# The moving tiles of a weight-stream kernel, stored as even and odd tokens and read in turn

## The chip, the cores and the metric

The kernel runs on one core of a Trainium2 chip. The metric is the device time of one execution, in microseconds. Three runs of the kernel before are shown, with a median of 1940.2 us. One execution was taken by the hardware profiler; all rows of the profile come from it.

The core has five instruction queues that matter here: TensorE (PE, with its weight loads listed as PEld), VectorE (DVE), ScalarE (ACT), GpSimd (POOL) and SyncE (SP), which issues most DMAs.

## The reference

One inference step of one decoder layer, for a prompt of 256 tokens and eight sample tokens of one step each. All is float32. Cut to the products with the large weights:

```python
mod = silu(c) @ w_ada + b_ada                      # 2048 -> 6 x 2048
h = rmsnorm(x) * (1 + sc1) + sh1
z = h @ w_in                                       # 2048 -> 15376
y_a = spatial_gating(u, v)                         # three mixers, each 1024 wide
y_b = head_rmsnorm(o_hg) * silu(hg)
y_c = head_rmsnorm(o_gla) * silu(gr)
merged = sum(sigmoid(z_gate[n]) * (y[n] @ w_branch[n]) for n in range(3))
x = x + gt1 * rmsnorm(merged @ w_out)
h2 = rmsnorm(x) * (1 + sc2) + sh2
x = x + gt2 * rmsnorm(square(relu(h2 @ w_mlp_up)) @ w_mlp_down)
```

The two mixers b and c are gated linear recurrences with states that are also outputs.

## The kernel before, in words

Activations are held with features on the 128 partitions and tokens along the free dimension. A block is a tile of 128 partitions x 4 feature groups x 264 tokens (`NT` = 256 prompt tokens, `NP`, and 8 samples, `NS`), made by `blk`. A product with a large weight takes a 128x128 piece of the weight as the stationary operand and 128x264 activations as the moving operand, and adds up in PSUM.

To be nearly exact, each float32 operand is split into a high part, rounded to the chip's fast float32 type (`F32R`), and a low part, the rest. `split` (lines 108 to 110) does this with a copy on Scalar and a subtraction on Vector. A product is then three: high weight x high activation, high weight x low activation, low weight x high activation (lines 643, 644 and 645, in `granule`).

The weights come as a stream. `plan` lists all pieces in the order of use, `Stream.load` issues their DMAs on SP into `raw` tiles (four buffers, with a few in `araw`), up to five pieces ahead. `Stream.split_half` splits them into `whi` and `wlo` (six buffers each), up to two pieces ahead. `granule` does the 24 products of one piece, and `background` then lets a share of the other work run: generators of the three mixers (`mixer_a`, `samples_r`, `mixer_r`), the modulation rows (`Rounds`), and work that was put off (`later`). The order on TensorE, and in some stages on other queues, is that of the program text.

The activations that the stream multiplies are split as follows:

- `modulate` (lines 425 to 453) makes `h` in pairs of feature groups and splits it into `hh` and `hl`. The first pair goes feature group by feature group, its samples on GpSimd (lines 430 to 434), its first prompt part on Vector (lines 447 and 448). `hH` and `hL` hand one feature group of it to `granule`.
- `yparts` (line 1308) splits the gated outputs of mixers a and b, `parts_c` (line 1363) those of mixer c.
- `branch` (line 1318) gates the projected mixers with tanh(z / 2) + 1, which is twice the sigmoid, and sums them in `mg`. The missing factor of 0.5 is put in when `mg` is split (lines 1337 and 1338).
- `quad` and `put_quad` (lines 1545 to 1580) make and split `h2`, its samples on GpSimd.
- `up` (line 1605) squares the positive part of the MLP's first product; its high part comes straight from Scalar's square (line 1616), its low part from Vector. `down` uses it one block of 1024 features later.

`tiles` (line 709) hands out the feature group `k` of a list of such blocks. Each moving operand is thus 264 tokens in a row, 1056 bytes on each partition:

```python
def tiles(bl):
    return lambda k: bl[k // 4][:, k % 4, :]
```

The factor of two of the other gates (`gate_tiles`, line 1342) is made good in the norm gains `hgnT` and `glanT`, which are multiplied by 0.5 at the start (line 163).

Of the kernel before, what the change touches and what calls it, by code (L numbers as in the profile page):

```python
# [57 lines left out]
def hybrid_step_kernel(  # L58
# [40 lines left out]
    def mul(o, a, b):  # L99
        V.tensor_tensor(o, a, b, op=ALU.mult)  # L100
# [7 lines left out]
    def split(src, hi, lo):  # L108
        S.copy(hi, src)  # L109
        sub(lo, src, hi.bitcast(F32))  # L110

    order = tc.manual_schedule(engines={mybir.EngineType.PE, mybir.EngineType.SP, mybir.EngineType.Pool})
    order.__enter__()

# [43 lines left out]
    def small_vectors():  # L158
        ps = sm()
        T.transpose(ps[:, 0:128], st1, ident)  # L160
        T.transpose(ps[:, 128:128 + n2], st2[0:n2, :], ident[0:n2, 0:n2])
        V.tensor_copy(vec, ps[:, 0:128 + n2])
        V.tensor_scalar(vec[:, 172:175], vec[:, 172:175], 0.5, None, ALU.mult)

    badaT = vec[:, 0:96]
    gpreT, gpostT = vec[:, 96:112], vec[:, 112:128]
# [258 lines left out]
    def modulate(dst, src, xs, k0, n, A, B, hi, lo):  # L425

        d = dst[:, :, NP:NT]
        one = k0 == 0
        if one:
            Q = nc.gpsimd  # L430
            Q.tensor_tensor(d, xs[:, k0:k0 + n, :], A[:, k0:k0 + n, 1:NC], op=ALU.mult)
            Q.tensor_tensor(d, d, B[:, k0:k0 + n, 1:NC], op=ALU.add)
            Q.tensor_copy(hi[:, :, NP:NT], d)
            Q.tensor_tensor(lo[:, :, NP:NT], d, hi[:, :, NP:NT].bitcast(F32), op=ALU.subtract)
        else:
            mul(d, xs[:, k0:k0 + n, :], A[:, k0:k0 + n, 1:NC])
            add(d, d, B[:, k0:k0 + n, 1:NC])
        for j in range(n):
            k = k0 + j
            if j % 2 == 0:  # L440
                V.tensor_scalar(dst[:, j, 0:NP], src[:, j, :], A[:, k, 0:1], B[:, k, 0:1], ALU.mult, ALU.add)
            else:
                S.activation(dst[:, j, 0:NP], src[:, j, :], AF.Identity, scale=A[:, k, 0:1], bias=B[:, k, 0:1])
            if one:
                p, h, l = (b[:, j, 0:NP] for b in (dst, hi, lo))
                if j == 0:
                    V.tensor_copy(h, p)
                    sub(l, p, h.bitcast(F32))
                else:
                    split(p, h, l)  # L450
            elif j % 2 == 1:
                js = slice(j - 1, j + 1)
                split(dst[:, js, :], hi[:, js, :], lo[:, js, :])

    hh, hl = [], []
    A1 = const([P, KT, NC], "A1")
# [250 lines left out]
        return acc[:, 0:width // P, 0:NT]  # L707

    def tiles(bl):
        return lambda k: bl[k // 4][:, k % 4, :]  # L710

    def pair(b, g):
        return b[:, 2 * g:2 * g + 2, :]

    def hH(k):
        return hh[k // 4][:, k % 4, :]

    def hL(k):
        return hl[k // 4][:, k % 4, :]

    win = w_in[0]

# [142 lines left out]
    def mixer_a():  # L865
        lng, lnb, wsr, bsb = consts_a
        lng, lnb = (v.rearrange("p g n -> p (g n)") for v in (lng, lnb))
        vtk = [blk([P, BW]), blk([P, BW])]
        yield from rows_of(vF, lambda t, g: vtk[t][:, g * CW:(g + 1) * CW])
        wsT = blk([P, 8, P])  # L870
        w00 = tmp([P, 8], "w00", 1)
        for gg in range(2):
            ps = sm()
            for i in range(4):
                T.transpose(ps[:, i * P:(i + 1) * P], wsr[:, 4 * gg + i, :], ident)
            yield
            mul(wsT[:, 4 * gg:4 * gg + 4, :], ps.rearrange("p (g n) -> p g n", g=4), triu.unsqueeze(1).to_broadcast([P, 4, P]))
        yield READY
        ps = sm()
        T.matmul(ps[:, 0:8], ones[0:1, :], wsT[0:1, :, 0:1].rearrange("p g o -> p (g o)"), start=True, stop=True)  # L880
        V.tensor_copy(w00, ps[:, 0:8])
        yield
        for v in vtk:
            st = tmp([P, 2, 6], "bst", 1)
            for i in range(2):
                V.bn_stats(st[:, i, :], v[:, i * 512:(i + 1) * 512])
            ag = tmp([P, 2], "bag", 1)
            V.bn_aggr(ag, st)
            rs = tmp([P, 1], "lnr", 1)
            rstd_small(ag[:, 1:2], 1.0, rs)  # L890
            yield
            V.tensor_scalar(v, v, ag[:, 0:1], rs, ALU.subtract, ALU.mult)
            yield
            mul(v, v, lng)
            yield
            add(v, v, lnb)
            yield

        vs = tmp([P, 8, NS], "vsa", 1)
        w8 = tmp([P, 8, NS], "vsb", 1)  # L900
        r8 = tmp([P, NS], "vsr", 1)
        for i in range(2):
            V.tensor_copy(vs[:, 4 * i:4 * i + 4, :], vF[i][:, :, NP:NT])
        V.tensor_copy(w8, vs)
        fold(w8, 8)
        yield READY
        ps = sum_partitions(w8, NS)
        yield 0.3
        V.tensor_scalar(r8, ps, 1.0 / BW, None, ALU.mult)
        sub(vs, vs, r8.unsqueeze(1).to_broadcast([P, 8, NS]))  # L910
        mul(w8, vs, vs)
        fold(w8, 8)
        yield 0.3
        yield READY
        ps = sum_partitions(w8, NS)
        yield 0.1
        rstd_small(ps, 1.0 / BW, r8)
        mul(vs, vs, r8.unsqueeze(1).to_broadcast([P, 8, NS]))
        mul(vs, vs, lngT.unsqueeze(2).to_broadcast([P, 8, NS]))
        add(vs, vs, lnbT.unsqueeze(2).to_broadcast([P, 8, NS]))  # L920
        V.tensor_copy(srow[:, 0:8, :].rearrange("p k b -> p (k b)").rearrange("p (b k) -> p k b", k=8), vs)
        yield 0.9
        yield READY
        yield READY
        ps = sm([P, P])
        T.transpose(ps, srow.rearrange("p k b -> p (k b)"), ident)
        so = tmp([64, P], "sqs", 1)
        S.copy(so, ps[0:64])
        nc.gpsimd.dma_start(sgu_v_sample[0].rearrange("b o (k p) -> (b o k) p", p=P), so)
        ys = tmp([P, 8, NS], "vsb", 1)  # L930
        mul(ys, vs, w00.unsqueeze(2).to_broadcast([P, 8, NS]))
        add(ys, ys, bsb[:, :, 0:1].to_broadcast([P, 8, NS]))
        for i in range(2):
            u = uT[i][:, :, NP:NT]
            mul(u, ys[:, 4 * i:4 * i + 4, :], u)
        yield 0.8
        for gp in range(4):
            ps = sm()
            for i in range(2):
                g = 2 * gp + i  # L940
                for c in range(2):
                    T.matmul(ps[:, (2 * i + c) * P:(2 * i + c + 1) * P], vtk[c][:, g * P:(g + 1) * P], wsT[:, g, :], start=True, stop=True)
            u = pair(uT[gp // 2], gp % 2)
            yv = tmp([P, 2, NT], "vt")
            yield
            add(
                yv[:, :, 0:NP].rearrange("p g (c n) -> p g c n", c=2),
                ps.rearrange("p (g c n) -> p g c n", g=2, c=2),
                bsb[:, 2 * gp:2 * gp + 2, :].unsqueeze(2).to_broadcast([P, 2, 2, P]),
            )  # L950
            mul(u[:, :, 0:NP], yv[:, :, 0:NP], u[:, :, 0:NP])
            yield
    order = tc.manual_schedule(engines={mybir.EngineType.PE, mybir.EngineType.Pool})
    order.__enter__()
# [353 lines left out]
    def yparts(ys):  # L1308
        h, l = [], []
        for y in ys:  # L1310
            a, b = blk(dt=F32R), blk(dt=F32R)
            split(y, a, b)
            h.append(a)
            l.append(b)
            bg.owed -= 0.8
        return tiles(h), tiles(l)

    def branch(n, parts):
        for m in range(8):
# [14 lines left out]
                add(dst, dst, gt)  # L1334
            if n == 2 and m % 2 == 1:
                a, b = blk(dt=F32R), blk(dt=F32R)
                S.activation(a, mg[m // 2], AF.Copy, scale=0.5)
                V.scalar_tensor_tensor(b, mg[m // 2], 0.5, a.bitcast(F32), ALU.mult, ALU.subtract)
                mh.append(a)
                ml.append(b)  # L1340

# [21 lines left out]
    def parts_c(gates):  # L1363
# [3 lines left out]
        for j, o in enumerate(Gs[2].o):  # L1367
# [1 line left out]
                g = gates[hd // 2][:, 2 * (hd % 2) + j, :]  # L1369
                V.scalar_tensor_tensor(o[:, hd, :], o[:, hd, :], glanT[:, j:j + 1], g, ALU.mult, ALU.mult)  # L1370
            a, b = blk(dt=F32R), blk(dt=F32R)
            split(o, a, b)
            h.append(a)
            l.append(b)
            bg.owed -= 0.8
        return (lambda k: h[k % 2][:, k // 2, :]), (lambda k: l[k % 2][:, k // 2, :])

    rate[:] = RATES[1]
    branch(0, parts_a)
# [164 lines left out]

    def quad(q):

        hs, ls = (h[q][:, :, NP:NT] for h in (h2h, h2l))
        Q.tensor_copy(hs, xa[:, 4 * q:4 * q + 4, :])
        Q.tensor_tensor(ls, xa[:, 4 * q:4 * q + 4, :], hs.bitcast(F32), op=ALU.subtract)
        for i2 in range(2):  # L1550
            if q > 0:
                ps = sm([P, 2, NP])
# [18 lines left out]
    def put_quad(q, i2, i, src, vt):  # L1571
# [5 lines left out]
        if q == 0 or i == 1:  # L1577
            a = i if q == 0 else 0
            js = slice(2 * i2 + a, 2 * i2 + i + 1)
            split(vt[:, a:i + 1, 0:NP], h2h[q][:, js, 0:NP], h2l[q][:, js, 0:NP])  # L1580

    quad(0)
    residual(1)
# [21 lines left out]
    def up(f, zs=()):  # L1605
        ah, al = [], []
        for m in range(FB // CW):
# [5 lines left out]
                al.append(blk(dt=F32R))  # L1613
            a, b = pair(ah[-1], m % 2), pair(al[-1], m % 2)
            sq = tmp([P, 2, NT], "gt")
            S.activation(a, rl, AF.Square)
            mul(sq, rl, rl)
            sub(b, sq, a.bitcast(F32))
        return tiles(ah), tiles(al)

    y2 = [blk() for _ in range(4)]
# [123 lines left out]
```

## Time and profile before

| | before |
|---|---|
| median of 3 runs | 1940.2 us |
| lowest and highest run | 1939.84 and 1943.49 us |
| span of the profiled execution | 1941.0 us |
| mean granted TensorE clock | 0.998 |
| products with 264 columns | 3 x 4624 |
| HBM read and written | 427.60 and 11.70 MB |

The page gives no time around the span, so the span is taken as the profiled execution's own time; it lies between the lowest and the highest run. A group's row reads: line, engine, operation, output<-inputs, shapes, count | busy time in us, mean ns of one | idle time of the engine before them and what ended it. Products overlap in the array, so the mean of one is not the distance to the next. A row of stretches reads: from:to, length, then busy time and count on TensorE, its weight loads, Vector, Scalar and GpSimd, then the granted clock, the mean share of the DMA engines and GB/s. A row in order of time reads: start, duration, engine, line, operation and how many instructions were merged into it.

### The profile page before, as it was taken

The page shows a single profiled execution, that of the slowest core. Times are in us where ns is not written, and L with a number is a line of the kernel's source. Part 1 is how long each engine was busy: PE and PEld are TensorE (multiplying, and loading weights), DVE is VectorE, ACT ScalarE, POOL GpSimd, SP SyncE. Part 2 cuts the span into 40 slices and gives each one's busy share as a digit, 9 for nine tenths or more (in the row PEclk, how much of TensorE's full clock was granted, in tenths as well). Part 3 has the DMA queues.
Part 4 walks back from the last instruction along what each step waited for, and adds up shares of the span by engine and source line. Part 5 has one row for each costly group of instructions (what it writes and reads, how often), then busy time and mean ns, then how long its engine had stood idle before and what let it go on. Part 6 is the DMA issues. An engine that isn't in the chain of part 4 may idle for free.

```text
span 1941.0 us, 42183 instructions
## 1 busy us (share of the span) xinstructions
PE 1906.3 (98%) x17012; PEld 1815.6 (94%) x17012; DVE 1186.7 (61%) x2092; ACT 1002.7 (52%) x1818; POOL 130.9 (7%) x210
## 2 busy tenths in 40 slices
PE   6999999999999999999999999999999999999998
PEld 5899999999999989899999989999999999999997
DVE  4566667686676785555555666545556555555665
ACT  5434354665855755544444555444444545454544
POOL 4311000001101111100000010000000000000000
PEclk9999999999999999999999999999999999999999
DMA  9987696788777778877777846776556556555552
GB/s 338 372 303 252 193 299 205 226 263 258 232 253 243 235 254 265 288 257 249 259 247 234 304 131 201 233 228 196 177 182 184 179 180 184 177 183 180 180 184 100
DMA packets 330179, 442.05 MB, mean 228 GB/s; under 512 B 14946, under 2 KB 276944, under 8 KB 329984
## 3 DMA queue, kind: packets, MB, share of 16 engines
q1 hardware_dynamic: 311728, 380.26, 61.7%
q0 software_dynamic: 17184, 57.85, 8.5%
q8 instruction: 133, 2.18, 0.5%
q10 hardware_dynamic: 1072, 1.25, 0.2%
q14 instruction: 62, 0.51, 0.1%
HBM read 427.60 MB, written 11.70 MB: 226 GB/s over the span
## 4 chain that ended last, share of the span: by engine, by line
PE 93%; DMA 3%; DVE 1%; issue 1%; ACT 1%; SPq 0%; POOL 0%; DVEq 0%; ACTq 0%; POOLq 0%
PE mm L643 28%; PE mm L644 28%; PE mm L645 28%; PE ada L362 3%; DMA raw<-in_w_in_dram 1%; PE ada L294 1%; DMA vbc<-vs_d 1%; PE sm L835 1%; PE sm L663 1%; DVE wlo L106 1%; PE sm L1192 1%; PE sm L670 1%; DMA b<-in_x_prompt_dram 0%; PE sm L1562 0%; DMA b<-in_w_ada_dram 0%
## 5 line engine op out<-in xcount | busy, mean ns | idle before, releaser
L643 PE MATMUL mm<-b,whi 128*128 128x264 f32 x4624 | 1326.4, 287 | 8.3 <-issue 2.4
L645 PE MATMUL mm<-b,wlo 128*128 128x264 f32 x4624 | 1313.1, 284 | 3.9 <-DVE wlo L106 3.6
L644 PE MATMUL mm<-b,whi 128*128 128x264 f32 x4624 | 1314.3, 284 | 0.6 <-DVE b L106 0.5
L106 DVE TENSOR_TENSOR wlo<-raw,whi 128x512 fp32r<-128x512 f32 x1136 | 776.9, 689 | 568.4 <-ACT whi L109 564.9
L109 ACT CAST whi<-raw 128x512 fp32r<-128x512 f32 x1136 | 696.2, 618 | 750.9 <-PE mm L644 669.2
L643 PEld LDWEIGHTS mm<-b,whi 128*128 128x128 f32 x4624 | 870.7, 188 | 49.6 <-issue 28.2
L645 PEld LDWEIGHTS mm<-b,wlo 128*128 128x128 f32 x4624 | 870.5, 188 | 5.1 <-DVE wlo L106 5.1
L644 PEld LDWEIGHTS mm<-b,whi 128*128 128x128 f32 x4624 | 871.0, 188 | 2.8 <-issue 1.4
L103 DVE TENSOR_TENSOR b<-b,mm 128x528 f32<-128x528 f32 (+1 forms) x137 | 95.7, 699 | 40.2 <-PE mm L645 39.9
L1089 DVE SCALAR_TENSOR_TENSOR st<-vbc,b,st 128x128 f32<-128x128 f32 (+1 forms) x96 | 34.1, 390 | 62.2 <-DMA vbc<-vs_d 57.4
L1087 ACT ACTIVATE st<-st,fs 128x128 f32<-128x128 f32 (+1 forms) x96 | 37.1, 431 | 56.4 <-DMA st<-in_state_hgrn_dram 28.6
L472 POOL DMA_DIRECT2D b<-in_w_ada_dram x64 | 46.2, 724 | 132.4 <-PE ada L294 101.3
L362 PE MATMUL ada<-araw,cT 128*32 128x512 f32 x296 | 39.8, 601 | 0.0
L294 PE MATMUL ada<-b,cT 128*32 128x256 f32 (+1 forms) x640 | 34.9, 354 | 1.8 <-DMA b<-in_w_ada_dram 1.5
L100 DVE TENSOR_TENSOR b<-b,b 128x512 f32<-128x512 f32 (+1 forms) x47 | 33.8, 740 | 1.3 <-ACT b L1205 1.1
L1090 POOL DMA_DIRECT2D out_dram<-st x32 | 23.5, 736 | 130.0 <-DVE st L1089 130.0
L294 PEld LDWEIGHTS ada<-b,cT 128*32 128x32 f32 x640 | 17.7, 113 | 14.3 <-DMA b<-in_w_ada_dram 5.3
L362 PE MATMUL ada<-b,cT 128*32 128x512 f32 x216 | 26.2, 593 | 0.0
L106 DVE TENSOR_TENSOR b<-gt,b 128x528 fp32r<-128x528 f32 x32 | 22.7, 708 | 3.2
L106 DVE TENSOR_TENSOR b<-b 128x1024 f32<-128x1024 f32 (+1 forms) x24 | 24.3, 1015 | 0.0
L109 ACT CAST whi<-araw 128x512 fp32r<-128x512 f32 x20 | 12.3, 620 | 21.0 <-PE mm L644 17.6
L100 DVE TENSOR_TENSOR gt<-vt 128x528 f32<-128x528 f32 x32 | 22.5, 702 | 0.9 <-ACT vt L1610 0.9
(346 smaller groups left out, 859.1 us busy)
## 6 DMA issues: line engine op xcount, KB each, us to landing
raw<-in_w_in_dram SPq DMA_DIRECT2D x231, 512.0 KB, 4.6
raw<-in_w_mlp_up_dram SPq DMA_DIRECT2D x128, 512.0 KB, 3.9
raw<-in_w_mlp_down_dram SPq DMA_DIRECT2D x128, 512.0 KB, 3.6
araw<-in_w_ada_dram SPq DMA_DIRECT2D x74, 512.0 KB, 5.4
b<-in_w_ada_dram SPq DMA_DIRECT2D x54, 512.0 KB, 5.5
b<-in_w_ada_dram POOLq DMA_DIRECT2D x48, 512.0 KB, 8.0
raw<-in_w_branch_dram SPq DMA_DIRECT2D x48, 512.0 KB, 4.5
raw<-in_w_out_dram SPq DMA_DIRECT2D x32, 512.0 KB, 4.0
```

What stands on the lines that cost most here:

```text
L100: V.tensor_tensor(o, a, b, op=ALU.mult)
L103: V.tensor_tensor(o, a, b, op=ALU.add)
L106: V.tensor_tensor(o, a, b, op=ALU.subtract)
L109: S.copy(hi, src)
L294: T.matmul(acc[32 * j:32 * j + 32, 0:n], cT[:, k, :], w[:, n * j:n * j + n], start=k == 0, stop=k == KT - 1)
L362: T.matmul(self.acc[32 * j:32 * j + 32, :], cT[:, k, :], ws[j // 2][:, j % 2 * 512:j % 2 * 512 + 512], start=k == 0, stop=k == KT - 1)
L472: queue.dma_start(w[:, i], w1[k * P:(k + 1) * P, :, self.k0 * P:(self.k0 + self.n) * P])
L643: T.matmul(o, a, xh(k + j), start=first and j == 0, stop=False)
L644: T.matmul(o, a, xl(k + j), start=False, stop=False)
L645: T.matmul(o, b, xh(k + j), start=False, stop=last and j == n - 1)
L1087: S.activation(st[:, i, :], st[:, i, :], AF.Copy, scale=fs[:, h0 + i, b:b + 1])
L1089: V.scalar_tensor_tensor(st[:, i, :], v[:, i, :], k[:, h0 + i, NP + b:NP + b + 1], st[:, i, :], ALU.mult, ALU.add)
```

## The change

A moving tile's 264 tokens are stored in two halves of 132 words: the even tokens, then the odd ones. `apart` views a stored tile as its two halves, `by_two` views a source by even and odd tokens, and `split_tokens` splits a source of natural order into parts stored that way. `moving` gives the products a view that takes a token from the first half and one from the second half in turn, so the columns of a product, and what it writes to PSUM, have the order of before. Tokens 0 to 255 and the samples fill columns 0 to 127 and 128 to 131 of each half.

All makers of moving parts write this way. Weights, their split and all sources stay as they are. Since the split of `mg` no longer scales, its 0.5 is moved ahead: into the gated values of mixer a (the products become a product of three factors, one of them 0.5) and into `hgnT` and `glanT` (0.25 in place of 0.5). `up` takes its high part with the same views.

```diff
+    def apart(v):
+        return v.rearrange("p n (r c) -> p n r c", r=2)
+
+    def by_two(v):
+        return v.rearrange("p n (c r) -> p n r c", r=2)
+
+    def moving(v):
+        return v.rearrange("p (r c) -> p c r", r=2)
+
+    def split_tokens(src, hi, lo, t0=0, t1=NT):
+
+        cs = slice(t0 // 2, t1 // 2)
+        split(by_two(src), apart(hi)[:, :, :, cs], apart(lo)[:, :, :, cs])
...
-        V.tensor_scalar(vec[:, 172:175], vec[:, 172:175], 0.5, None, ALU.mult)
+        V.tensor_scalar(vec[:, 172:175], vec[:, 172:175], 0.25, None, ALU.mult)
...
-            Q.tensor_copy(hi[:, :, NP:NT], d)
-            Q.tensor_tensor(lo[:, :, NP:NT], d, hi[:, :, NP:NT].bitcast(F32), op=ALU.subtract)
+            hs, ls = (apart(b)[:, :, :, NP // 2:NT // 2] for b in (hi, lo))
+            Q.tensor_copy(hs, by_two(d))
+            Q.tensor_tensor(ls, by_two(d), hs.bitcast(F32), op=ALU.subtract)
...
-                p, h, l = (b[:, j, 0:NP] for b in (dst, hi, lo))
+                p = by_two(dst[:, j:j + 1, 0:NP])
+                h, l = (apart(b[:, j:j + 1, :])[:, :, :, 0:NP // 2] for b in (hi, lo))
...
-                split(dst[:, js, :], hi[:, js, :], lo[:, js, :])
+                split_tokens(dst[:, js, :], hi[:, js, :], lo[:, js, :])
...
     def tiles(bl):
-        return lambda k: bl[k // 4][:, k % 4, :]
+        return lambda k: moving(bl[k // 4][:, k % 4, :])
...
     def hH(k):
-        return hh[k // 4][:, k % 4, :]
+        return moving(hh[k // 4][:, k % 4, :])
...
-            mul(u, ys[:, 4 * i:4 * i + 4, :], u)
+            V.scalar_tensor_tensor(u, ys[:, 4 * i:4 * i + 4, :], 0.5, u, ALU.mult, ALU.mult)
...
-            mul(u[:, :, 0:NP], yv[:, :, 0:NP], u[:, :, 0:NP])
+            V.scalar_tensor_tensor(u[:, :, 0:NP], yv[:, :, 0:NP], 0.5, u[:, :, 0:NP], ALU.mult, ALU.mult)
...
-            split(y, a, b)
+            split_tokens(y, a, b)
...
-                S.activation(a, mg[m // 2], AF.Copy, scale=0.5)
-                V.scalar_tensor_tensor(b, mg[m // 2], 0.5, a.bitcast(F32), ALU.mult, ALU.subtract)
+                split_tokens(mg[m // 2], a, b)
...
-        hs, ls = (h[q][:, :, NP:NT] for h in (h2h, h2l))
-        Q.tensor_copy(hs, xa[:, 4 * q:4 * q + 4, :])
-        Q.tensor_tensor(ls, xa[:, 4 * q:4 * q + 4, :], hs.bitcast(F32), op=ALU.subtract)
+        hs, ls = (apart(h[q])[:, :, :, NP // 2:NT // 2] for h in (h2h, h2l))
+        xq = by_two(xa[:, 4 * q:4 * q + 4, :])
+        Q.tensor_copy(hs, xq)
+        Q.tensor_tensor(ls, xq, hs.bitcast(F32), op=ALU.subtract)
...
-            split(vt[:, a:i + 1, 0:NP], h2h[q][:, js, 0:NP], h2l[q][:, js, 0:NP])
+            split_tokens(vt[:, a:i + 1, 0:NP], h2h[q][:, js, :], h2l[q][:, js, :], 0, NP)
...
-            S.activation(a, rl, AF.Square)
+            S.activation(apart(a), by_two(rl), AF.Square)
             mul(sq, rl, rl)
-            sub(b, sq, a.bitcast(F32))
+            sub(apart(b), by_two(sq), apart(a).bitcast(F32))
```

More of the change, by code (lines that the diff above doesn't have):

```diff
@@ L715, in hH @@
     def hH(k):
-        return hh[k // 4][:, k % 4, :]
+        return moving(hh[k // 4][:, k % 4, :])
     def hL(k):
-        return hl[k // 4][:, k % 4, :]
+        return moving(hl[k // 4][:, k % 4, :])
     win = w_in[0]
@@ L1371, in parts_c @@
             a, b = blk(dt=F32R), blk(dt=F32R)
-            split(o, a, b)
+            split_tokens(o, a, b)
             h.append(a)
@@ L1375, in parts_c @@
             bg.owed -= 0.8
-        return (lambda k: h[k % 2][:, k // 2, :]), (lambda k: l[k % 2][:, k // 2, :])
+        return (lambda k: moving(h[k % 2][:, k // 2, :])), (lambda k: moving(l[k % 2][:, k // 2, :]))
     rate[:] = RATES[1]
```

## The prediction

> **What bounds the kernel now.** I read the page's first line, its busy shares, the slices and the chain of work first, then the stretches of time, then the order of time on TensorE.
>
> ```profile
> span 1941.0 us, 42183 instructions
> PE 1906.3 (98%) x17012; PEld 1815.6 (94%) x17012; DVE 1186.7 (61%) x2092; ACT 1002.7 (52%) x1818; POOL 130.9 (7%) x210
> PEclk9999999999999999999999999999999999999999
> PE 93%; DMA 3%; DVE 1%; issue 1%; ACT 1%; SPq 0%; POOL 0%; DVEq 0%; ACTq 0%; POOLq 0%
> L643 PE MATMUL mm<-b,whi 128*128 128x264 f32 x4624 | 1326.4, 287 | 8.3 <-issue 2.4
> L645 PE MATMUL mm<-b,wlo 128*128 128x264 f32 x4624 | 1313.1, 284 | 3.9 <-DVE wlo L106 3.6
> L644 PE MATMUL mm<-b,whi 128*128 128x264 f32 x4624 | 1314.3, 284 | 0.6 <-DVE b L106 0.5
> ```
>
> TensorE is 93% of the chain, the granted clock is full in every slice, and three lines carry nearly all of it: 3 x 4624 = 13,872 products. All three read a moving tile of 264 tokens (`b`), which is just what the change stores anew. Their 284 to 287 ns overlap, so what counts is the distance from one start to the next. In the second half of the kernel nothing but these products runs on TensorE, and it never waits:
>
> ```profile
> 1400.00:1600.00 200.00, 200.00 (x1649) 200.00 (x1649) 116.11 (x172) 93.48 (x154) 0.00 (x0) 1.00 0.59 181
> ```
>
> So one product takes 200.00 / 1649 = 121.3 ns, or 0.459 ns a column, with Vector and Scalar busy for 116 and 93 of 200 us and the DMA engines for 59%. The order of time shows the same step product by product:
>
> ```profile
> 1400.07 0.28 PE L643 MATMUL mm<-b,whi 128*128 128x264 f32 x1
> 1400.19 0.28 PE L644 MATMUL mm<-b,whi 128*128 128x264 f32 x1
> 1400.31 0.29 PE L645 MATMUL mm<-b,wlo 128*128 128x264 f32 x1
> 1400.44 0.29 PE L643 MATMUL mm<-b,whi 128*128 128x264 f32 x1
> 1400.57 0.28 PE L644 MATMUL mm<-b,whi 128*128 128x264 f32 x1
> 1336.99 0.28 PE L643 MATMUL mm<-b,whi 128*128 128x264 f32 x1
> 1337.10 0.28 PE L644 MATMUL mm<-b,whi 128*128 128x264 f32 x1
> ```
>
> The step is 0.11 to 0.13 us although shape, type and clock are the same every time. Only the places in memory differ, of the moving tile and of the weights that are loaded meanwhile. For scale, two rows of plain float32 products with 512 columns:
>
> ```profile
> 1928.60 1.02 PE L1668 MATMUL mm<-b,cst 128*128 128x512 f32 x2
> 1929.46 0.50 PE L1451 MATMUL sm<-cst,a 128*128 128x1 f32 x4
> 1334.29 1.07 PE L362 MATMUL ada<-araw,cT 128*32 128x512 f32 x8
> 1335.18 1.04 PE L362 MATMUL ada<-b,cT 128*32 128x512 f32 x8
> ```
>
> Two passes of 512 columns take 1929.46 - 1928.60 = 0.86 us, 0.84 ns a column. The fast type of the weight stream stands at 0.459, a little over half of it. If it streams at just half, 264 columns take 264 x 0.42 = 111 ns, and 10 ns of the 121.3 are not the array's columns but something about the reads. The second pair shows eight instructions, four side by side in the array, which read from four places of two `araw` tiles, in 1335.18 - 1334.29 = 0.89 us: as long as one product alone. Memory can serve TensorE from several places at once.
>
> **The change part by part.**
>
> (1) The moving read, 13,872 times. Instructions on all five queues stay the same in number and order; only views change (and a few scalings, below). The step becomes x instead of 121.3 ns. The trace has no product whose columns come in turn from two places 528 bytes apart (132 tokens of 4 bytes), so I bound x. Below: 111 ns. Above: 264 x 0.84 = 222 ns, the pace of the plain float32 row, at which a column may take two reads. In between, one row shows what leaving a contiguous order can cost, on Vector: the sum that writes 128 values 16 words apart against a product of the same size in order:
>
> ```profile
> 1932.86 0.28 DVE L100 TENSOR_TENSOR gs<-gs,nr 128x128 f32<-128x128 f32 x1
> 1933.72 0.37 DVE L103 TENSOR_TENSOR sqs<-gs,xsT 128x128 f32<-128x128 f32 x1
> ```
>
> That is 0.37 / 0.28 = 1.32 times as long; the same ratio on a product gives 121.3 x 1.32 = 160 ns. So the rows reach from 111 over 160 to 222. I take 114 ns: the row nearest in kind is TensorE's own from four places at once, which shows no loss, and the scatter of 0.11 to 0.13 us by place says that the contiguous order loses something to where it reads; two alternating places should spread that. The shortest steps in the order of time, 0.11, lie about there.
>
> Not all products gain. In the first 160 us the stream comes as fast as the DMA engines give it:
>
> ```profile
> 0.00:160.00 160.00, 82.78 (x282) 53.67 (x283) 0.99 0.93 333
> 160.00:1941.00 1781.00, 1243.58 (x4342) 817.06 (x4342) 1.00 0.69 218
> ```
>
> (These rows are of line 643 alone.) There the engines are 93% busy at 333 GB/s, so I give nothing. Behind it lie 3 x 4342 = 13,026 products at a DMA share of 0.69: 13,026 x (121.3 - 114) = 95 us. What is late next: per 12 products Scalar casts once and Vector subtracts once.
>
> ```profile
> L106 DVE TENSOR_TENSOR wlo<-raw,whi 128x512 fp32r<-128x512 f32 x1136 | 776.9, 689 | 568.4 <-ACT whi L109 564.9
> L109 ACT CAST whi<-raw 128x512 fp32r<-128x512 f32 x1136 | 696.2, 618 | 750.9 <-PE mm L644 669.2
> 400.00:600.00 200.00, 198.60 (x2377) 185.07 (x2376) 140.80 (x279) 128.48 (x265) 26.77 (x40) 1.00 0.79 256
> ```
>
> 12 x 114 = 1.37 us against 0.62 and 0.69 us, so the split keeps up, and its longest waits today are for TensorE. In the mixer stretch Vector is at 140.80 of 200 us and the DMA share at 0.79; 6% more pace gives 0.75 and 0.84. I take 4 us off for waits there: 91 us stay.
>
> [...]
>
> (2) The split into parts (`split_tokens`, `quad`, `modulate`, `up`, `branch`). Reads now take every second word, writes run in two halves.
>
> ```profile
> L1616 ACT ACTIVATE b<-vt 128x528 fp32r<-128x528 f32 x32 | 20.7, 647 | 1.0
> L106 DVE TENSOR_TENSOR b<-gt,b 128x528 fp32r<-128x528 f32 x32 | 22.7, 708 | 3.2
> L1158 ACT ACTIVATE b<-b 128x512 f32<-128x512 f32 x3 | 2.1, 696 | 1.6 <-DVE b L106 1.6
> L1153 ACT ACTIVATE b<-b 128x512 f32<-128x512 f32 x12 | 7.6, 637 | 0.0
> L106 DVE TENSOR_TENSOR b<-b 128x512 f32<-128x512 f32 x9 | 6.1, 683 | 0.0
> L447 DVE CAST b<-b 128x256 fp32r<-128x256 f32 x1 | 0.3, 294 | 0.0
> L106 DVE TENSOR_TENSOR b<-b,b 128x256 fp32r<-128x256 f32 x2 | 0.8, 426 | 0.0
> ```
>
> Line 1158 reads and writes every second word: 696 against 637 ns, 59 ns more on Scalar. Vector's subtractions of 128x512, three of whose nine (those of line 1157) read every second word, cost no more than others. Some 60 Scalar instructions (32 squares of `up`, the rest of the parts) x 0.06 = 3.6 us, and nothing on Vector. `up` runs a block ahead of its `down`, so the weight stream covers it; without cover it would cost those 3.6 us. On the path lie the first split at the start and the four of `quad(0)`: the copy of line 447 may fall from 294 to the 426 ns of a subtraction, and five Scalar copies gain 0.06 each: 0.13 + 0.3 = 0.4 us.
>
> (3) The scaling by 0.5, moved from the merged tiles into the gated values, the two norm gains and six products of `mixer_a`:
>
> ```profile
> L1338 DVE SCALAR_TENSOR_TENSOR b<-b,b 128x1056 fp32r<-128x1056 f32 x4 | 5.0, 1259 | 1.5 <-ACT b L1337 1.5
> L106 DVE TENSOR_TENSOR b<-b,b 128x1056 fp32r<-128x1056 f32 x6 | 7.5, 1248 | 0.0
> ```
>
> 11 ns between the two forms, ten times, in both directions: nothing.
>
> (4) GpSimd's parts of the eight samples keep their sizes (line 433 and `quad`) and lie beside TensorE: nothing, at most 1 us.
>
> Sum: 1941.0 - 91 + 0.4 = 1850 us. The profiled span is 0.8 us above the median of 1940.2, and the page shows no time around the span, so I forecast 1850.
>
> **The rivals.**
>
> Half pace (slower): each column opens a new place, and a product streams like a plain float32 pass: 222 ns. It decides as soon as the step is above 121.3; at 222 it is 13,872 x 100.7 = 1397 us more, 3337 us, with Vector and Scalar half idle. For it: the contiguous order is the only one TensorE has shown at 0.46 ns a column, and the four simultaneous reads of line 362 run at 0.84 each, so they have slack that these lack. Against: those four reads together fetch more per ns than one fast one. A part of it, the Vector ratio (160 ns), gives 13,872 x 38.7 = 537 us more: 2477 us.
>
> No difference: the step does not depend on the order of places at all, only on a fixed cost of some 10 ns per product for changing weights. Then only (2) is left, 0.4 to 4 us: 1941 to 1944. For it: the step is 0.12 in the loaded first stage and the quiet last one alike. Against: the scatter by place.
> [...]
>
> **How the numbers follow.** Faster, 0.47: steps of 111 to 121 ns, times from 1941 - 13,026 x 10.3 / 1000 = 1807 up to 1936, most of it in 1820 to 1920; this case's own range. No difference, 0.08. Slower, 0.45: half pace 0.27, in between (by way of 160 ns) 0.18. A change of 0.2% (4 us) is about what a measurement of this kernel can tell. Half pace holds more than 2 in 10, so the range must reach it: 1815 to 3345; it leaves out only the best of the first case. The predicted time is that of the likeliest case, 1850.
>
> **What would show it.** For (1): the count of products in any 200 us behind 1200; 1649 now, 1754 at 114 ns, 901 at 222, and steps in the order of time that scatter less. Lines 643 to 645 keep 4624 each. For (2): Scalar's squares at some 0.70 instead of 0.65 us, Vector's subtractions unchanged at 0.71. For (3) and (4): no new waits of TensorE for Vector or GpSimd. The prediction is wrong if the step is not below 121, or if it is and waits for `whi`, `wlo` or raw tiles take the gain back.

## The result and the profile after

| | before | after |
|---|---|---|
| median of 4 runs each | 1941.16 us | 1835.93 us |
| lowest and highest run | 1939.84 and 1943.49 us | 1832.18 and 1836.85 us |
| span of the profiled execution | 1941.0 us | 1830.4 us |

The ratio is 0.9457, with a 95% interval from 0.9444 to 0.9471. The forecast was 1850 us. It had the direction, and it took the gain 14 us too small. Why it came out so is weighed below.

The page of the kernel after, its first line, busy shares, chain and the three groups of products (each line moved down by 16, so lines 643 to 645 are now 659 to 661):

```profile
span 1830.4 us, 42186 instructions
PE 1788.7 (98%) x17012; PEld 1696.5 (93%) x17012; DVE 1181.8 (65%) x2092; ACT 1000.3 (55%) x1818; POOL 131.3 (7%) x210
PE 88%; DMA 2%; DVE 2%; issue 1%; ACT 1%; POOL 0%; DVEq 0%; ACTq 0%; POOLq 0%
L659 PE MATMUL mm<-b,whi 128*128 128x264 f32 x4624 | 1292.4, 279 | 12.3 <-issue 5.1
L661 PE MATMUL mm<-b,wlo 128*128 128x264 f32 x4624 | 1279.7, 277 | 5.1 <-DVE wlo L106 4.5
L660 PE MATMUL mm<-b,whi 128*128 128x264 f32 x4624 | 1278.8, 277 | 0.8 <-DVE b L106 0.7
```

There are still 3 x 4624 products, and TensorE still carries the chain, with 88% instead of 93%. The idle time in front of the first two groups has grown by 5 us. The stretches of time show where the gain lies; the columns are those of the stretches before:

```profile
0.00:160.00 160.00, 139.20 (x1407) 120.99 (x1411) 89.31 (x180) 75.82 (x131) 45.50 (x73) 0.99 0.94 336
400.00:600.00 200.00, 195.28 (x2323) 181.54 (x2323) 141.55 (x274) 131.79 (x274) 27.32 (x41) 0.99 0.80 261
1400.00:1600.00 200.00, 200.00 (x1781) 200.00 (x1780) 125.32 (x186) 100.35 (x164) 0.00 (x0) 1.00 0.65 196
```

From 1400 to 1600 us, where nothing but products runs, there are 1781 instead of 1649: 200.00 / 1781 = 112.3 ns for one, against 121.3. In the mixer stretch, 400 to 600 us, TensorE is now idle for 4.7 of 200 us, where it was idle for 1.4. In order of time the step hardly scatters any more:

```profile
1399.96 0.28 PE L659 MATMUL mm<-b,whi 128*128 128x264 f32 x1
1400.07 0.28 PE L660 MATMUL mm<-b,whi 128*128 128x264 f32 x1
1400.18 0.28 PE L661 MATMUL mm<-b,wlo 128*128 128x264 f32 x1
1400.30 0.28 PE L659 MATMUL mm<-b,whi 128*128 128x264 f32 x1
```

All steps are 0.11 or 0.12 us, where the kernel before had 0.11 to 0.13. Over all undisturbed products of the two traces, from one start to the next, the spread (standard deviation) fell from 2.9 to 0.5 ns.

Scalar pays for the new places. The groups of its splits, with shapes kept apart, first before:

```profile
L109 ACT CAST b<-b 128x1056 fp32r<-128x1056 f32 x6 | 6.5, 1076 | 0.4 <-PE sm L663 0.3 <-DVE b L1360 0.2
L109 ACT CAST b<-vt 128x512 fp32r<-128x512 f32 x6 | 3.7, 621 | 0.2
```

and after, with the squares of `up` (line 1616 before, 647 ns) and two of Vector's groups:

```profile
L1632 ACT ACTIVATE b<-vt 128x528 fp32r<-128x528 f32 x32 | 23.0, 719 | 1.0
L109 ACT CAST b<-b 128x1056 fp32r<-128x1056 f32 x10 | 12.1, 1209 | 1.1 <-DVE b L1375 0.7
L109 ACT CAST b<-vt 128x512 fp32r<-128x512 f32 x6 | 4.0, 673 | 0.2
L106 DVE TENSOR_TENSOR b<-gt,b 128x528 fp32r<-128x528 f32 x32 | 22.7, 710 | 3.2
L106 DVE TENSOR_TENSOR b<-b,b 128x1056 fp32r<-128x1056 f32 x10 | 12.5, 1254 | 2.5 <-ACT b L109 2.5
```

The squares take 719 instead of 647 ns, the large casts 1209 instead of 1076. Vector's subtractions are as long as before (708 and 1248 ns).

### The profile page after: what moved, and what is told of

The parts are those of the page before. It is cut to its first block, busy times and chain, and to the rows that moved or that the text cites. A ratio compares the mean times of both kernels' runs of the same rounds, so it can differ in the third digit from the quotient of the medians.

```text
span 1830.4 us, 42186 instructions
## 1 busy us (share of the span) xinstructions
PE 1788.7 (98%) x17012; PEld 1696.5 (93%) x17012; DVE 1181.8 (65%) x2092; ACT 1000.3 (55%) x1818; POOL 131.3 (7%) x210
## 4 chain that ended last, share of the span: by engine, by line
PE 88%; DMA 2%; DVE 2%; issue 1%; ACT 1%; POOL 0%; DVEq 0%; ACTq 0%; POOLq 0%
PE mm L659 27%; PE mm L661 26%; PE mm L660 26%; PE ada L376 3%; DMA vbc<-vs_d 1%; PE ada L308 1%; DVE wlo L106 1%; PE sm L851 1%; PE sm L1208 1%; PE sm L679 1%; PE sm L686 1%; DMA raw<-in_w_in_dram 0%; DVE b L106 0%; PE sm L1578 0%; ACT whi L109 0%
## 5 line engine op out<-in xcount | busy, mean ns | idle before, releaser
L659 PE MATMUL mm<-b,whi 128*128 128x264 f32 x4624 | 1292.4, 279 | 12.3 <-issue 5.1
L661 PE MATMUL mm<-b,wlo 128*128 128x264 f32 x4624 | 1279.7, 277 | 5.1 <-DVE wlo L106 4.5
L660 PE MATMUL mm<-b,whi 128*128 128x264 f32 x4624 | 1278.8, 277 | 0.8 <-DVE b L106 0.7
L1632 ACT ACTIVATE b<-vt 128x528 fp32r<-128x528 f32 x32 | 23.0, 719 | 1.0
L106 DVE TENSOR_TENSOR b<-b,b 128x1056 fp32r<-128x1056 f32 (+3 forms) x21 | 20.8, 991 | 4.0 <-ACT b L109 3.8
```

The costliest lines, as they stand in the source:

```text
L106: V.tensor_tensor(o, a, b, op=ALU.subtract)
L659: T.matmul(o, a, xh(k + j), start=first and j == 0, stop=False)
L660: T.matmul(o, a, xl(k + j), start=False, stop=False)
L661: T.matmul(o, b, xh(k + j), start=False, stop=last and j == n - 1)
```

## The experiments

### The two halves of the change

The first kernel stores as the change does, but reads in order of address; the second leaves the storage alone and only reads in turn.

```diff
 # store only: after, with
     def moving(v):
-        return v.rearrange("p (r c) -> p c r", r=2)
+        return v
```

```diff
 # read only: before, with
+    def moving(v):
+        return v.rearrange("p (r c) -> p c r", r=2)
+
     def tiles(bl):
-        return lambda k: bl[k // 4][:, k % 4, :]
+        return lambda k: moving(bl[k // 4][:, k % 4, :])
...
```

The cut stands for the same change in `hH`, `hL` and `parts_c`.

> The changed kernel, but the products read each moving tile in the order in which it lies: the even tokens, then the odd ones (so every result column stands for another token, and the outputs with it). The writes of the change stay, its reads go. Theory (the order of the reads alone sets the step): the step of a product is back at 121.4 ns and the time at 1941 to 1945 us. Rival (the new places or the new writes bring the gain): a step near 112.5 ns and a time near 1836 us.

> The kernel before, with nothing changed but the view by which the products read: a token from the first half and one from the second half in turn, from tiles stored in natural order (so result columns stand for other tokens). Theory (order of the reads): a step of 112.5 ns and 1832 to 1837 us, a little less than the changed kernel, since Scalar's 60 ns per split are saved. Rival (places or writes): 121.4 ns and 1941 us.

| | median | ratio to before | 95% interval |
|---|---|---|---|
| store only (10 runs) | 1942.43 us | 1.0015 | 1.0004 to 1.0025 |
| read only (4 runs) | 1830.23 us | 0.9426 | 0.9407 to 0.9444 |
| before beside them (13 runs) | 1939.88 us | | |

The last stretch, 1400 to 1600 us, of store only:

```profile
1400.00:1600.00 200.00, 200.00 (x1650) 200.00 (x1649) 116.09 (x172) 93.98 (x154) 0.00 (x0) 1.00 0.58 181
```

and of read only:

```profile
1400.00:1600.00 200.00, 200.00 (x1780) 200.00 (x1779) 125.24 (x186) 99.92 (x164) 0.00 (x0) 1.00 0.62 196
400.00:600.00 200.00, 196.19 (x2329) 182.33 (x2328) 142.83 (x277) 133.34 (x277) 27.30 (x41) 0.99 0.81 263
```

The whole gain belongs to the order of the read: 200 / 1650 = 121.2 ns for a product with the new storage alone, 200 / 1780 = 112.4 with the new order alone. Storage by itself costs 1940 x 0.0015 = 2.9 us, from 0.8 to 4.9. Read only is also 5.7 us below the full change by medians, but these come from different series, and the two profiled spans (1829.0 and 1830.4 us) differ by 1.4 us. The writes thus cost something between 1 and 6 us. The idle time in the mixer stretch is there in read only too (200 - 196.19 = 3.8 us), so it isn't the writes that cause most of it.

### Does the distance between the two places matter?

The MLP's products run in eight stretches of 768, each with another view of 256 moving columns; the two places are 8 to 512 bytes apart. The first and the last product of each accumulation group keep the order of address, at least 264 columns and all 128 weight columns, here and in the following experiments. This kernel and the following ones were run once each, so only stretches of one execution are compared.

```diff
...
+        (None, 256, 128, 1),
+        (('p (a r c) -> p a c r', {'r': 2, 'c': 128}), 256, 128, 1),
+        (('p (a r c) -> p a c r', {'r': 2, 'c': 64}), 256, 128, 1),
...
+        (('p (a r c) -> p a c r', {'r': 2, 'c': 4}), 256, 128, 1),
+        (('p (a r c) -> p a c r', {'r': 2, 'c': 2}), 256, 128, 1),
...
```

> The kernel before; in the MLP alone, eight stretches of 768 products read 256 columns (the eight samples are left out) in eight ways: in order, then in turn from two places 512, 256, 128, 64, 32, 16 and 8 bytes apart. Free of stalls a product of 256 columns would take 109 ns (the 112.5 ns of the changed kernel less 8 columns), in order some 118. Theory (the moving read and the loading of the next weights meet in the same part of memory, and reading in turn leaves gaps for the other): 109 at the distances whose two places lie in different parts, no gain at those that fall into the same part (512 and 256 bytes, if the parts repeat every 256 bytes). Rival (it is enough that neighbouring columns do not come from one 16-byte line): 109 from 512 down to 16 bytes, and 118 at 8 bytes alone.

Five stretches: in order of address, then in turn 512, 128, 16 and 8 bytes apart:

```profile
1200.00:1250.00 50.00, 50.00 (x423) 46.86 (x422) 27.49 (x42) 24.50 (x41) 0.00 (x0) 1.00 0.73 235
1300.00:1350.00 50.00, 50.00 (x446) 48.44 (x446) 28.33 (x43) 26.77 (x45) 0.00 (x0) 1.00 0.67 215
1440.00:1490.00 50.00, 50.00 (x447) 50.00 (x446) 30.92 (x46) 22.95 (x38) 0.00 (x0) 1.00 0.63 197
1700.00:1750.00 50.00, 50.00 (x448) 50.00 (x447) 30.54 (x45) 22.97 (x38) 0.00 (x0) 1.00 0.61 192
1800.00:1850.00 50.00, 50.00 (x426) 50.00 (x425) 32.73 (x57) 24.73 (x43) 0.00 (x0) 1.00 0.57 183
```

50 us by the counts gives 118.2, 112.1, 111.9, 111.6 and 117.4 ns. From 512 down to 16 bytes the distance does not matter (111.6 to 112.1 ns). At 8 bytes, where both places lie in the same 16 bytes and only the order within them is 0, 2, 1, 3, nearly all of the gain is gone (117.4 ns). So the idea that two far places are served by two parts of the memory falls: places 16 bytes apart do just as well. Neither side's 109 ns was reached. The experiment with the weights, below, shows a floor of 111 to 112 ns for products with 128 weight columns, so a difference of 2 or 3 ns between the distances could not have shown here.

### Other orders

Again eight stretches of 768 products, now of 264 columns.

```diff
...
+        (('p (r c q) -> p c r q', {'r': 2, 'q': 2}), 264, 128, 1),
+        (('p (r c q) -> p c r q', {'r': 2, 'q': 4}), 264, 128, 1),
+        (('p (c r) -> p r c', {'r': 2}), 264, 128, 1),
...
+        (('p (r c) -> p c r', {'r': 4}), 264, 128, 1),
+        (('p (r c) -> p c r', {'r': 8}), 264, 128, 1),
...
```

> The kernel before; in the MLP alone, eight stretches of 768 products read their 264 columns in eight orders: two tokens in turn from each half, four tokens in turn from each half, every second token then the others (8 bytes a step), every fourth (16 bytes a step), every twelfth (48 bytes a step), in turn from four quarters, in turn from eight eighths, in turn from two halves. Theory (meeting of two streams): every order that leaves a place after one column gives 112.5 ns, four in turn stays near 121, two in turn lies between. Rival (a 16-byte line gives its columns too slowly by itself): 112.5 wherever neighbours are in different lines, and 8 bytes a step as well as two in turn about half way, 117.

Two tokens in turn from each half, four in turn, every second token, every twelfth, four quarters in turn, eight eighths in turn:

```profile
1200.00:1250.00 50.00, 50.00 (x303) 48.32 (x302) 20.32 (x30) 18.36 (x30) 0.00 (x0) 1.00 0.53 168
1320.00:1370.00 50.00, 50.00 (x384) 48.40 (x383) 22.66 (x33) 22.44 (x37) 0.00 (x0) 1.00 0.66 215
1450.00:1500.00 50.00, 50.00 (x221) 44.02 (x220) 14.91 (x22) 11.14 (x18) 0.00 (x0) 1.00 0.32 96
1850.00:1900.00 50.00, 50.00 (x160) 47.80 (x159) 10.54 (x16) 8.50 (x14) 0.00 (x0) 0.57 0.22 70
2020.00:2070.00 50.00, 50.00 (x356) 50.00 (x355) 24.83 (x37) 19.18 (x32) 0.00 (x0) 1.00 0.49 153
2150.00:2200.00 50.00, 50.00 (x227) 45.10 (x226) 16.22 (x24) 11.76 (x19) 0.00 (x0) 1.00 0.31 95
```

These are 165, 130, 226, 312, 140 and 220 ns (the products at the ends of a group, which read in order of address, are in these means; the median product takes 170, 131, 236, 320, 142 and 230). Both theories written down for this run fall: no order that leaves a place after one column, other than two halves in turn, came near 112.5 ns. Every second token takes 236 ns, about twice the 112.5 of the best order, although neighbours still share 16 bytes two by two. That gave the author's next theory, worked out from these times alone: count the even and the odd columns of a product apart (two of the expectations below call each of the two a lane), and what matters is how often each of them comes to other 16 bytes. In order of address two even columns, or two odd ones, lie in each 16 bytes (121 ns), with two halves in turn four (112.5), with every second token one (236). The row of every twelfth token isn't comparable: the granted clock was 0.57 there.

### Do the weights have a part in it?

The kernel before lost 9 ns, and its step depended on places. One explanation was that the reads of the next weights meet the reads of the columns.

```diff
...
+        (None, 264, 128, 1),
+        (None, 264, 32, 1),
+        (None, 264, 64, 1),
+        (None, 264, 128, 4),
+        (('p (r c) -> p c r', {'r': 2}), 264, 128, 4),
+        (None, 132, 128, 1),
+        (('p (r c) -> p c r', {'r': 2}), 132, 128, 1),
...
+                        a, b = a[:, 0:m1], b[:, 0:m1]
+                        if step > 1:
+                            a, b = (p.rearrange("p n w -> p (n w)")[:, 0:step * P:step] for p in parts[j // h])
...
```

> The MLP's 6,144 products (but for the first and last of each accumulation group) are run in eight stretches of 768, and the values of the MLP are wrong by it: (0) 264 moving columns in order of address, 128 weight columns; (1) the same with 32 weight columns; (2) with 64; (3) with 128 weight columns that lie 16 bytes apart (every fourth word of the stored weights); (4) as (3) with the moving columns of the two halves in turn; (5) 132 moving columns in order; (6) 132 in turn; (7) 264 in turn, 128 plain weight columns. Theory: the 9 ns that a product loses in order of address are lost where its reads meet the reads of the next product's weights, and in turn they have room. Then (0) is 121 ns, (1) 112 to 115, (2) 114 to 118, (3) above 125, (4) 113 to 116, (7) 112.5. Rival: the 9 ns belong to the order of the moving read by itself, and the weights have nothing to do with it: (0), (1), (2) and (3) all 120 to 122, (4) and (7) both 112 to 113. For half the columns: if the time is a time per column, (5) is 60 ns and (6) 56; if 112 ns is a floor that a change of 128 weight columns sets, both stay above 100 ns and are equal.

Stretches 0, 1, 3, 4, 5 and 6:

```profile
1200.00:1250.00 50.00, 50.00 (x413) 46.84 (x412) 26.57 (x40) 23.48 (x40) 0.00 (x0) 1.00 0.70 229
1300.00:1350.00 50.00, 50.00 (x417) 43.59 (x414) 25.96 (x40) 24.58 (x41) 0.00 (x0) 1.00 0.65 210
1500.00:1550.00 50.00, 50.00 (x222) 50.00 (x223) 15.12 (x23) 11.17 (x18) 0.00 (x0) 1.00 0.31 95
1700.00:1750.00 50.00, 50.00 (x221) 50.00 (x220) 15.17 (x23) 12.91 (x21) 0.00 (x0) 1.00 0.31 95
1820.00:1870.00 50.00, 50.00 (x449) 50.00 (x447) 31.28 (x47) 25.07 (x42) 0.00 (x0) 1.00 0.64 199
1910.00:1960.00 50.00, 50.00 (x448) 50.00 (x447) 30.68 (x46) 24.99 (x41) 0.00 (x0) 1.00 0.64 195
```

With a quarter of the weight columns the contiguous product still takes 50 / 417 = 119.9 ns against 121.1, where the theory of colliding weights wanted 112 to 115. It falls: the 9 ns belong to the moving read. Weights 16 bytes apart behave as neither side expected: 50 / 222 = 225 ns in order and 226 in turn (the median product 234 and 233). There the weight load seems to set the step: one load's row in the trace rises from 188 to 330 ns, the order of the moving read no longer matters, and the step is 234 / 128 = 1.8 ns a weight column. And with half the moving columns, both orders take 111 to 112 ns: a change of 128 weight columns is a floor at about that. With 32 weight columns the same 132 columns take 61 and 58 ns (below, in the last experiment). The changed kernel's 112.3 ns thus lies right at this floor, but the floor is not what holds it there: with 32 weight columns its 264 columns still take 112.

### Even and odd columns counted apart

```diff
...
+        lambda b4, v: b4.rearrange("p n t -> p (n t)")[:, 1:265],
+        lambda b4, v: v.rearrange("p (r c) -> p c r", r=6),
+        lambda b4, v: b4.rearrange("p n t -> p (n t)")[:, 0:528].rearrange("p (r c s) -> p c r s", r=2, s=2)[:, :, :, 0],
+        lambda b4, v: b4.rearrange("p n t -> p (n t)")[:, 0:1056].rearrange("p (r c s) -> p c r s", r=2, s=4)[:, :, :, 0],
+        lambda b4, v: b4.rearrange("p n t -> p (n t)")[:, 0:792].rearrange("p (r c s) -> p c r s", r=2, s=3)[:, :, :, 0],
+        lambda b4, v: v[:, 0:1].to_broadcast([P, NT]),
...
```

> The MLP's products again in eight stretches of 768 with other orders of the 264 moving columns (its values are wrong by it): (0) in order of address, but begun one word later, so that pairs of columns straddle 8-byte limits; (1) six places 176 bytes apart in turn; (2) two places 1056 bytes apart in turn, each taking every second word; (3) the same, 2112 bytes apart, every fourth word, so that each column is alone in its 16 bytes; (4) two places 1188 words' bytes apart, every third word; (5) one word for all columns; (6) two halves in turn, next words; (7) in order of address. Theory of two lanes (even and odd columns are fetched each by a lane of its own, and a lane is at full pace with four columns of the same 16 bytes one after the other, nearly so with two, and at half pace with one): (1) 150 to 200 ns, for each lane meets three places in turn; (2) 118 to 125, two columns for each 16 bytes in a lane; (3) about 240; (4) 150 to 190; (5) 112; (6) 112.5; (7) and (0) 121. Rival, that only the count of different 16-byte pieces that are wanted within a short stretch of columns matters, and two are best: (2), (3) and (4) 112 to 116 like (6), (1) 160 to 230, (5) 121 like (7).

In (4) the two places are in fact 396 words, or 1584 bytes, apart. All eight stretches in order:

```profile
1200.00:1250.00 50.00, 50.00 (x404) 46.83 (x403) 26.08 (x40) 22.74 (x38) 0.00 (x0) 1.00 0.69 223
1300.00:1350.00 50.00, 50.00 (x339) 47.80 (x341) 19.28 (x29) 19.77 (x33) 0.00 (x0) 1.00 0.58 184
1420.00:1470.00 50.00, 50.00 (x425) 50.00 (x424) 29.17 (x43) 25.16 (x42) 0.00 (x0) 1.00 0.60 185
1550.00:1600.00 50.00, 50.00 (x219) 44.23 (x218) 15.02 (x22) 12.29 (x20) 0.00 (x0) 1.00 0.31 96
1700.00:1750.00 50.00, 50.00 (x288) 50.00 (x287) 19.35 (x30) 16.00 (x26) 0.00 (x0) 1.00 0.41 125
1810.00:1860.00 50.00, 50.00 (x443) 50.00 (x442) 30.56 (x45) 24.63 (x42) 0.00 (x0) 1.00 0.63 196
1900.00:1950.00 50.00, 50.00 (x445) 50.00 (x444) 30.46 (x45) 25.71 (x43) 0.00 (x0) 1.00 0.62 195
2000.00:2050.00 50.00, 50.00 (x416) 50.00 (x415) 34.92 (x71) 26.34 (x50) 0.00 (x0) 1.00 0.41 132
```

The counts give 124, 147, 118, 228, 174, 113, 112 and 120 ns; the median products take 124, 152, 118, 236, 178, 112, 113 and 121. The rival wanted 112 to 116 for the third, fourth and fifth stretch, which all read just two places in turn; it falls. The theory gave ranges for the third and the fifth that hold 118 and 178, and about 240 for the fourth. There the even columns lie in one of the two places and the odd ones in the other, in steps of 8, 16 and 12 bytes. So each of the two comes to new 16 bytes at every second of its columns, at every one, and at three of four: 132, 264 and 198 times in all for 264 columns. 118 / 132, 236 / 264 and 178 / 198 are all 0.89 to 0.90 ns for one such change. The start one word later costs 3 ns (124 instead of 121), which neither side expected.

What this does not explain: with two tokens in turn from two halves, six places, or four quarters, the even columns change places at every one of them, and so do the odd ones; at 0.89 ns for each of 264 changes that would be 235 ns, and eight eighths do take 230. But these products take 170, 152 and 142. Four tokens in turn from two halves bring two even and two odd columns from each 16 bytes, as the order of address does, and take 131 ns instead of 121. So the count fits some orders and misses others. No trace shows how the columns are fetched; the two lanes are the author's reading of these times.

### The pace by columns

```diff
...
+        (264, 32, True),
+        (132, 32, False),
+        (132, 32, True),
+        (396, 128, False),
+        (396, 128, True),
+        (512, 128, False),
+        (512, 128, True),
...
```

The numbers are moving columns, weight columns, and whether the columns come in turn.

> The MLP's products in eight stretches of 768 with other numbers of columns (its values are wrong by it): (0) 264 moving columns in turn, 32 weight columns; (1) 132 in order of address, 32 weight columns; (2) 132 in turn, 32; (3) 396 in order, 128; (4) 396 in turn, 128; (5) 512 in order, 128; (6) 512 in turn, 128; (7) 264 in turn, 128. Theory: a product takes the longest of three: 112 ns for a change of 128 weight columns (the 111 and 112 ns of 132 columns), about 0.417 ns for each moving column (110 ns, the least that 264 columns took in turn), and 0.92 ns for each 16-byte piece that a lane of even or odd columns has to fetch (121 ns for the 132 of 264 columns in order; in turn there are half as many). Then (0) 110, (1) 61, (2) 55 to 58, (3) 182, (4) 165, (5) 235, (6) 213, (7) 112.5. Rival: the order adds a fixed time to a product, 9 ns whatever its columns: (3) 174 against (4) 165, (5) 222 against (6) 213, (1) 64 against (2) 55. Second rival: a column has no pace of its own and the pieces alone count, so that in turn 396 and 512 columns are no slower than the change of weights: (4) and (6) 112 to 120.

Stretches 3 to 6 (396 in order and in turn, 512 in order and in turn):

```profile
1420.00:1470.00 50.00, 50.00 (x280) 50.00 (x279) 20.02 (x30) 15.44 (x25) 0.00 (x0) 1.00 0.41 120
1580.00:1630.00 50.00, 50.00 (x300) 50.00 (x299) 20.18 (x30) 17.64 (x29) 0.00 (x0) 1.00 0.42 127
1700.00:1750.00 50.00, 50.00 (x220) 40.96 (x219) 15.05 (x23) 11.56 (x19) 0.00 (x0) 1.00 0.32 97
1900.00:1950.00 50.00, 50.00 (x233) 43.58 (x232) 15.73 (x24) 13.63 (x23) 0.00 (x0) 1.00 0.34 103
```

Median products, stretch by stretch: 112, 61, 58, 180, 167, 228, 216 and 113 ns. From 132 to 512 columns in turn the time grows by (216 - 58) / 380 = 0.416 ns a column, in order by (228 - 61) / 380 = 0.439. The second rival (no pace per column) falls with 167 and 216. The first, a fixed 9 ns, wanted a difference of 9 ns at every width; by the medians it is 3, 8, 13 and 12 ns at 132, 264, 396 and 512 columns (that at 264 is from the experiment before, 121 against 113), so the loss grows with the columns, though not evenly. The theory's price for each piece made 512 columns in order too dear: 235 ns expected, 228 measured. The theory's 110 ns for 264 columns beside 32 weight columns came out as 112, so 2 to 3 ns come on top of the columns.

## Why the prediction was right

**(1) The moving read.** One step of the reasoning held: some 10 of the 121.3 ns are not the array's columns but belong to the contiguous read, and reading in turn gets them back. The taken step of 114 ns was too large; it is 112.3, close to the lower bound of 111. 13,026 products x (121.3 - 112.3) = 117 us instead of 95.

Why reading in turn gets them back was said wrongly: it was to spread the reads over two places. Two places 8 bytes apart gain next to nothing (117.4 ns against 118.2), two places 16 bytes apart gain as much as 512 (111.6 and 112.1), and two places in turn whose own steps are 8, 12 or 16 bytes take 118, 178 and 236 ns. Most of these rows fit a count of how often the even and the odd columns come to other 16 bytes, which the prediction did not consider. That the chosen order lay at the good end was therefore in part luck. The forecast also was not sure of the direction: it gave 0.47 to faster and 0.45 to slower, and its range, 1815 to 3345 us, would have held most outcomes.

The 114 ns were argued from two rows, and neither argument holds as it was meant. The plain float32 products read four places at once, but those are four products side by side; one product that takes its columns from four places in turn took 142 ns. And the scatter of the old steps was put down to the places of the weights too; with 32 weight columns the contiguous products took 120.8 ns in the mean and scattered by 2.6 ns, just as with 128 (121.5 and 2.6). So these runs show no part of the weights in that scatter. The rival "no difference" failed all the same: the 10 ns weren't a fixed cost of changing weights, for 9 of them go when only the order of the columns changes (112.4 ns in read only).

Read in turn, 132, 264, 396 and 512 columns took 58, 113, 167 and 216 ns (132 columns with 32 weight columns, the others with 128), 0.42 to 0.44 ns a column. No order tried took fewer than 112 ns for 264 columns: one word for all of them took 112 too. So it was the kernel before, at 121.3, that fell short of the best pace measured here, and the changed kernel, at 112.3, reaches it.

**What is late next.** 4 us were taken off for waits. Counted product by product, the gain is 3.2 us at product 864 (9.0 ns each would be 7.8), 19.9 at product 3000, 27.7 at product 4800, and 110.5 at the last. From 4800 on a product gains 9.1 ns on average. Between 3000 and 4800, the later mixer stretch from 468 to 742 us of the kernel before, 7.8 us come instead of 16.2: 8 us are given back there, and 2.5 more between 864 and 3000. From 400 to 640 us, the waits of TensorE's weight loads before:

```profile
PEld mm L643 <- ACT whi L109: 1.7, 2, 0.8
PEld mm L645 <- DVE wlo L106: 0.5, 2, 0.3
```

and after (us in all, times, longest):

```profile
PEld mm L659 <- ACT whi L109: 4.4, 6, 0.8
PEld mm L661 <- DVE wlo L106: 3.0, 7, 0.9
```

This is the split of the weights coming late, as the prediction named it, 5.2 us more of it in these rows; the term of 4 us was too small. That it is late because of the mixers' work on Scalar and Vector is likely but not shown. Another 2.7 us are something the prediction had no term for. Before the same two products of the stream (the 3802nd and the 4558th) TensorE stands still and the profile names no cause ("issue"), first in the kernel before, then after:

```profile
589.09 0.28 PE L643 MATMUL mm<-b,whi 128*128 128x264 f32 x1 [1.27 <-issue]
705.38 0.39 PE L643 MATMUL mm<-b,whi 128*128 128x264 f32 x1 [1.13 <-issue]
565.89 0.27 PE L659 MATMUL mm<-b,whi 128*128 128x264 f32 x1 [2.86 <-issue]
678.16 0.38 PE L659 MATMUL mm<-b,whi 128*128 128x264 f32 x1 [2.19 <-issue]
```

In all four of these cases, and in those of store only and read only, a 16 KB transfer of the queue that the page calls "q8 instruction" has ended 1.3 to 1.5 us before TensorE goes on. In the kernel after, these transfers begin at 563.5 and 675.9 us, and TensorE stands still from 563.0 and 676.0. That it waits here for its own program is the author's estimate from these times and is not shown; why the transfers come later is open. That the first 160 us would gain nothing holds nearly: they gain 3 us.

**(2) The splits.** The squares were said to rise from 0.65 to 0.70 us and rose to 0.72; Vector's subtractions stayed. Summed over its groups, 2.3 us of it the squares (32 x 0.072), Scalar does some 4.4 us more in these splits; 3.6 were worked out. Of this the prediction put 0.4 us on the path, 0.13 of it for the copy of line 447, which did not get dearer (295 ns, it was 294). Store only measured 2.9 (0.8 to 4.9), and the spans of the full change and of read only differ by 1.4. A small term, taken too small.

**(3) and (4).** The new subtractions of the merged tiles take 1254 ns where the scaled form took 1259; GpSimd's busy time is 131.3 us, it was 130.9. Nothing, as written.

With the measured terms the sum of the prediction reads 117 + 3 - 8 - 2.5 = 109.5 us, the writes being in what is given back, and the spans differ by 1941.0 - 1830.4 = 110.6. These terms are read off the same two traces, so that they add up is no proof of their causes.

**The rivals.** Half pace did not come here, yet other orders came to it: with every second token a product takes 236 ns, with two places each in steps of 16 bytes also. With the even and the odd columns counted apart, the number of them that come one after the other from the same 16 bytes goes with the time in most rows: four 112, two 118 to 121, one 236 ns. It does not fit four orders in which the even or the odd columns go back and forth between places (131, 142, 152 and 170 ns).

A kernel that reads in turn and spares the dearer writes, by putting the columns right when PSUM is emptied, could gain at most the 1 to 6 us by which read only lies below the change. It wasn't tried.

## What to carry to other kernels

Before a stream of products is taken to be at its bound, divide the distance between two starts by the columns. Here, on fast float32, 0.46 ns a column (121.3 ns for 264) meant that the moving operand was read in a poor order. Two places 528 bytes apart in turn, each read word by word, brought 0.43 (112.3 ns); with 256 columns, places 16 to 512 bytes apart brought 111.6 to 112.1 ns instead of 118.2. Test such an order by changing the read alone, even if the outputs then come out in another order: it takes one line and shows the gain free of what the storage costs. When a stage then speeds up by 7%, look for the stages in which some of the gain is lost: here 10.5 of some 120 us, 8 of them in the later mixer stretch.

## What was not expected of the hardware

- Reading the moving operand in order of address is not the fastest order: 121 ns for 264 columns, 112 to 113 with two halves in turn; with 256 columns, places just 16 bytes apart do as well (112 ns instead of 118).
- Columns in steps of 8 bytes cost nearly as much as in steps of 16 (236 and 240 ns for the median product); two places in turn, each in steps of 8 bytes, took 118.
- With weight columns 16 bytes apart a product of 264 columns takes 233 to 234 ns in either order, 1.8 ns a weight column.
- While the products took every twelfth token, the granted clock fell to 0.54 to 0.63, though TensorE was never idle; in the stretches before and behind it was 1.00. Why stays open.
